# Two transformer blocks on one core: scores of two heads at a time, bias rows made ahead, compressed keys read by stride, the last group by halves of the tokens

## The chip, the cores and the metric

The kernel runs on 1 core of a Trainium2 chip. The metric is the device time of one execution in microseconds (us), a median of 3 runs. Everything below is of that core: TensorE (PE) does the matmuls and transposes, VectorE (DVE) and ScalarE (ACT) the work between them, GpSimd (POOL) fills a few tiles, and SyncE (SP) issues the DMAs from the chip's memory.

## What is computed

Two transformer blocks over 256 tokens of width 2048, batch 1, all in float32. The first has sparse attention with 16 query heads of 64 columns and 4 key heads beside a causal convolution of 31 taps over 1024 channels, both projected by one output matrix, and then a feed-forward network. The second block (latent attention, gated linear attention, a feed-forward network with a gated residual) isn't touched but for its last additions. Cut to what the change touches:

```
def compress_tokens(tok, pos, w1, w2):         # blocks of 32 tokens, one every 16: 15 blocks
    blocks = blocks + pos                      # pos: 32 vectors of 64
    return silu(flat @ w1) @ w2                # flat: 15 x (32*64); w1 2048x64; w2 64x64

proj = rms_norm(x) @ w_in                      # q, kv (3 branches), gates, conv_in
k_cmp, v_cmp = compress_tokens(...)            # branch 0
# per query head, branch in (compressed, selected, window):
s = q @ k.T * 64**-0.5 + rel_bias[bucket(t - s)]      # masked to s <= t
o += gate[branch] * softmax(s) @ v
conv = silu(layer_norm(depthwise_conv31(a * sigmoid(gate))))
x = x + concat([attn, conv]) @ w_out           # then the feed-forward network
...
x = x + gate_f * rms_norm(f, g_post_ffn)       # the last line of the second block
```

With 256 tokens the selected blocks and the window both cover every earlier token, so each head has two score matrices of 256 x 256 (causal) and one of 256 x 15 against the compressed keys.

## The kernel before

**Weights.** The work is a list of groups (`GROUPS`): projections `c0, c1, kvc, c2, kk, gt, q0, q1, c3, vv, q2, q3`, then the output projection in `oa0` to `oa7` (rows of the first four pairs of heads), `ob0` to `ob7` (rows of the last four pairs) and `oz0` to `oz7` (rows of the convolution), then the feed-forward network and block 2. A group is walked in steps (`MCS`), one weight tile of 128 x 1024 each. A tile lands as `raw`, ACT rounds it to `wh`, DVE takes the remainder `wl`, and PE does three matmuls per block of 128 rows: `wh` with the high part of the input, `wh` with the low part, `wl` with the high part. `run_group` writes these, and they are called main matmuls below; a step of `oa` or `ob` has 24 of them.

**Order.** The program is written out once, by a planner in Python that keeps a modelled clock per engine. Between main matmuls `tick()` lets side generators write their next piece when its model says that their inputs are ready; `need(n)` makes a generator wait for n of the eight PSUM banks. Each engine then runs its list in that order, whatever the real times are. `conv_gen`, the convolution on DVE, is a side with low priority: it is written where the model has DVE to spare.

**The pieces that the change touches.**
- `bias_gen` (L948) makes the relative bias on the chip: a one-hot table `oht` is loaded, one matmul gives 16 rows of 384 distances (`tabr`, sent to `dtab` in memory, read back by `load_B` as a tile `B` per pair), and 15 matmuls of 16 columns give the bias of the compressed keys (`cbias`).
- `cmp_gen`: per key and value, DVE writes the blocks with the position vectors added (`blk`, 8 additions, the even and odd tokens of a block in the two halves of the partitions), and 16 matmuls of 128 rows by 60 columns give the hidden layer.
- `ev_kk` copies the keys into `kz`, one tile per key head, with zeros in the 64 partitions that belong to the other head of a query pair. `att_gen(n)` does head n: two score matmuls of 128 rows against `kz` into two banks (`S1`, `S0`) and two against `kcz`; then DVE adds the bias and takes the maximum (`add_max`), ACT takes the exponentials, DVE the reciprocal sums `rs`, ACT scales P by them, PE transposes P (8 transposes), ACT copies them out (`PT`), and for a pair together PE multiplies with V (`PT,vz` and `PT,V`), in two halves of 64 columns of the array. ACT and DVE then write the pair's `o` as high and low part. `att_driver` starts head n when the scores of head n-1 are written.
- A main matmul of `ob0` to `ob7` is written only when its rows of `o` are planned; the fourth row block of each step is that of the last pair. `oz` needs the convolution's end: `sd`, `R` (the LayerNorm's factors), `upad` (swish), `ch` and `cl`.
- `finish()` ends the program: for each half of the tokens DVE adds, scales and writes four blocks of 512 columns and sends each to `out`.

Of the kernel before, what the change touches and what calls it, by code (L numbers as in the profile page):

```python
# [13 lines left out]
F32 = mybir.dt.float32  # L14
# [9 lines left out]
T = 256  # L24
D = 2048
# [118 lines left out]
PB = 3  # L144
# [4 lines left out]
AHEAD = 2  # L149
SKIP = 48  # L150
# [43 lines left out]
OH = Layout([("ohr", 384), ("ohf", 512)])  # L194
CA = Layout([("mix_g", 16), ("ffn_g", 16), ("relb", 16), ("cmask", 32), ("conv_w", 248), ("conv_b", 8), ("ln_g", 8),
# [3 lines left out]
OFF_C = 271  # L199
# [14 lines left out]
def _onehot(dist, width):  # L214
    o = np.zeros((128, width), np.float32)
    i = np.arange(len(dist))
    o[_bucket(dist), i] = 1.0
    o[32, i] = dist < 0
    return o


def pack_small(inp):
# [21 lines left out]
    for tt in range(2):  # L244
        cm[:, tt, :15] = (16 * np.arange(15)[None] + 31) <= (tt * 128 + t)[:, None]
    relb = np.zeros((33, 16), np.float32)
    relb[:32] = f["rel_bias"][:, HORD]
    relb[32] = NEG
    pos = f["cmp_pos"][0]
    oh = put(OH, dict(ohr=_onehot(np.arange(384) - 127, 384), ohf=_onehot(np.arange(512) - OFF_C, 512)))  # L250
    ca = put(CA, dict(
        mix_g=cols(f["mix_norm_g"][0]), ffn_g=cols(f["ffn_norm_g"][0]), relb=relb,
        cmask=cm.reshape(128, 32), conv_w=f["conv_w"][0].reshape(31, 8, 128).transpose(2, 1, 0).reshape(128, 248),
# [21 lines left out]
    w1 = w1.reshape(2, 16, 128, 64).transpose(0, 2, 1, 3).reshape(2, 128, 1024)  # L275
# [5 lines left out]
    return dict(vec=vec, fv=fv, oh=oh, ca=ca, cb=cb, w1=c(w1), wada=c(wada), x=c(x), pos=c(f["positions_2"]))  # L281
# [92 lines left out]
class Kern:  # L374
    def __init__(self, nc, tc, a, dump=None, stop=None):
# [11 lines left out]
        self.hl = {}  # L387
# [164 lines left out]
    def run_group(self, g):  # L552
# [5 lines left out]
        src = self.src  # L558
# [10 lines left out]
        kl = len(g["ks"]) - 1  # L569
# [3 lines left out]
        for mi in g["mcs"]:  # L573
# [6 lines left out]
            h, l = self.next_mc(mi)  # L580
            t["PE"] = max(t["PE"], self.l_end.pop(mi))
            for u in range(nt if g["mode"] == "w" else 2):
                o = ps[u][:min(n, 128)] if g["mode"] == "w" else ps[u][:, :n]
                for q, k in enumerate(m["ks"]):
                    xh, xl = src(k, N)
                    if g["mode"] == "w":
                        c = slice(q * n + u * 128, q * n + u * 128 + min(n, 128))
                        p = ((h[:, c], xh), (h[:, c], xl), (l[:, c], xh))
                    else:
                        c, ts = slice(q * n, q * n + n), slice(u * 128, u * 128 + 128)  # L590
                        p = ((xh[:, ts], h[:, c]), (xl[:, ts], h[:, c]), (xh[:, ts], l[:, c]))
                    for i, (a, b) in enumerate(p):
                        self.mm(o[:, :b.shape[1]], a, b, k == 0 and i == 0, k == kl and i == 2)
                    if q % GRAN == GRAN - 1 and (u, k) != (nb - 1, m["ks"][-1]):
                        self.tick()
            self.emitted += 1
            if mi != g["mcs"][-1]:
                self.tick()
        ev = self.evac[key]
# [5 lines left out]
        self.tick()  # L605

# [127 lines left out]
    def build(self):  # L734
        nc, tc = self.nc, self.tc
        with ExitStack() as es:
# [10 lines left out]
            with ExitStack() as ph:  # L747
# [12 lines left out]
                if not self.stop:  # L760
                    self.finish()
# [26 lines left out]
    def block1_setup(self):  # L788
# [12 lines left out]
        self.kz = P.tile([128, 4, 2, T], F32, name="kz")  # L801
        self.V = P.tile([128, 2, 2, 4, 64], F32, name="V")
        self.Gt = P.tile([128, 2, 8, 2, 3], F32, name="Gt")
        self.cbias = P.tile([128, 2, 8, 2, 16], F32, name="cbias")
        self.kcz = P.tile([128, 4, 16], F32, name="kcz")
# [6 lines left out]
        g.memset(self.kz, 0.0)  # L812
        g.memset(self.kcz, 0.0)
        g.memset(self.vz, 0.0)
        g.memset(self.cbias, NEG)
# [26 lines left out]
        self.side(self.bias_gen())  # L842
# [105 lines left out]
    def bias_gen(self):  # L948
        while "ss" not in self.flags:
            yield  # L950
        oh = self.early.tile([128, OH.n], F32, name="oht", tag="g2")
        self.sy.dma_start(oh, self.a["oh"])
        ohr, ohf = (oh[:33, o:o + n] for o, n in OH.at.values())
        yield 8.0
        yield from self.need(1)
        o = self.bank()
        self.mm(o[:16, :384], self.ca("relb", 0, 16)[:33], ohr)
        yield
        tr = self.early.tile([16, 384], F32, name="tabr", tag="tok")
        self.act(tr, o[:16, :384], AF.Copy)  # L960
        self.free(o)
        self.dtab = self.dp.tile([16, 384], F32, name="dtab")
        self.sy.dma_start(self.dtab, tr)
        yield
        yield from self.need(1)
        bk = self.bank()
        o = bk[:, :256].rearrange("p (n h) -> p n h", n=16)
        for w in range(15):
            c = OFF_C - 31 + 128 - 16 * w
            self.mm(o[:, w], ohf[:, c:c + 128], self.ca("relb", 0, 16)[:33])  # L970
        yield

        for tt, w, n in ((0, 8, 7), (1, 0, 15)):
            self.v.tensor_copy(self.cbias[:, tt].rearrange("p a u n -> p (a u) n")[:, :, :n],
                               o[:, w:w + n].rearrange("p n h -> p h n"))
        self.free(bk)
# [1059 lines left out]
```

## Time and profile before

| what | value |
|---|---|
| median of the runs | 2206.18 us (2204.81 to 2206.24) |
| the profiled execution | 2205.54 us, its span 2203.8 us |
| PE | busy 2167.6 us, 98% of the span, 17465 records |
| DVE | busy 1692.8 us, 77% |
| ACT | busy 1179.5 us, 54% |
| DMA | 499.20 MB, 227 GB/s on average |

A busy time counts every record of an engine, so PE at 98% says that PE nearly always had something in it, not that it couldn't be given less. One fp32 matmul shows as two records, a main matmul as one. A group of equal records that follow each other is printed as one row with its count; its time reaches from the first start to the last end, and the ends of records overlap the next start by some 0.1 us, so what something costs PE is read from start to start. All rows name line 306, a helper that records each call, so pieces are told apart by their tiles.

### The profile page before, as it was taken

What the parts mean: (1) busy time and instruction counts of PE and PEld (TensorE: products, weight loads), DVE (VectorE), ACT (ScalarE), POOL (GpSimd) and SP (SyncE); (2) the same over time, 40 slices, a digit from 0 to 9 for tenths busy, and PEclk for the clock granted to TensorE, in tenths of its full rate; (3) what the DMA queues carried; (4) which work ended last, traced back from release to release, by engine and by line L of the source; (5) the groups of instructions that cost most, each with busy time, mean ns of one, the idle gap of its engine ahead of it and who ended that gap; (6) DMA issues with size and microseconds to landing.
All of it is one profiled execution on the core that took longest, in us unless ns stands there. A gap on an engine that the chain in (4) does not pass through costs nothing.

```text
span 2203.8 us, 42192 instructions
## 1 busy us (share of the span) xinstructions
PE 2167.6 (98%) x17465; PEld 2081.5 (94%) x17465; DVE 1692.8 (77%) x2611; ACT 1179.5 (54%) x1805; POOL 5.1 (0%) x18
## 2 busy tenths in 40 slices
PE   8999999999999999999999999999999999999997
PEld 7998889999999999999999889989998999899986
DVE  7998988999998699999988666678676665554455
ACT  5447686655553355555556664466444444444443
POOL 0000000000000000000000000000000000000000
PEclk9999999999999999999999999999999999999999
DMA  6554325788888788888855334646776775555553
GB/s 232 192 178 152 130 82 194 254 322 325 310 326 323 276 316 316 323 319 306 302 201 180 134 134 137 209 153 211 251 260 244 254 252 189 194 188 176 192 194 131
DMA packets 86784, 499.20 MB, mean 227 GB/s; under 512 B 9648, under 2 KB 12096, under 8 KB 40128
## 3 DMA queue, kind: packets, MB, share of 16 engines
q1 hardware_dynamic: 86592, 496.51, 63.6%
q8 instruction: 136, 2.23, 0.4%
q14 instruction: 56, 0.46, 0.1%
HBM read 494.35 MB, written 2.12 MB: 225 GB/s over the span
## 4 chain that ended last, share of the span: by engine, by line
PE 89%; DVE 6%; ACT 2%; issue 1%; DMA 1%; SPq 0%; DVEq 0%; ACTq 0%
PE ps L306 89%; DVE wl L306 2%; DMA raw<-in_wst_dram 1%; DVE cacc L306 1%; ACT wh L306 0%; DVE X L306 0%; DVE ac L306 0%; ACT L306 0%; DVE og L306 0%; ACT P L306 0%; DVE nt L306 0%; ACT X L306 0%; ACT ge L306 0%; DVE XT L306 0%; DVE ss L306 0%
## 5 line engine op out<-in xcount | busy, mean ns | idle before, releaser
L306 PE MATMUL ps<-X,wh 128*128 128x256 f32 (+1 forms) x7680 | 1330.3, 277 | 5.1 <-ACT X L306 2.9
L306 ACT ACTIVATE wh<-raw 128x1024 fp32r<-128x1024 f32 (+2 forms) x741 | 782.8, 1058 | 837.6 <-PE ps L306 781.2
L306 DVE TENSOR_TENSOR wl<-raw,wh 128x1024 fp32r<-128x1024 f32 (+2 forms) x741 | 898.9, 1215 | 393.8 <-PE ps L306 339.4
L306 PEld LDWEIGHTS ps<-X,wh 128*128 128x128 f32 x7680 | 1161.5, 188 | 11.4 <-ACT X L306 3.5
L306 PE MATMUL ps<-X,wl 128*128 128x256 f32 (+1 forms) x3840 | 1060.2, 276 | 4.8 <-DVE wl L306 4.8
L306 PEld LDWEIGHTS ps<-X,wl 128*128 128x128 f32 x3840 | 722.1, 188 | 6.0 <-DVE wl L306 6.0
L306 DVE SCALAR_TENSOR_TENSOR ac<-wa,cs,ac 128x512 f32<-128x512 f32 x360 | 269.5, 749 | 6.8
L306 PE MATMUL ps<-hid,wh 128*128 128x256 f32 x1408 | 239.5, 275 | 0.0
L306 PE MATMUL ps<-wh,hid 128*128 128x512 f32 x704 | 216.5, 388 | 0.0
L306 PEld LDWEIGHTS ps<-hid,wh 128*128 128x128 f32 x1408 | 212.0, 188 | 0.0
L306 PE MATMUL ps<-hid,wl 128*128 128x256 f32 x704 | 193.6, 275 | 0.0
L306 PEld LDWEIGHTS ps<-wh,hid 128*128 128x128 f32 x704 | 131.9, 188 | 27.4
L306 PE MATMUL ps<-wl,hid 128*128 128x512 f32 x352 | 136.6, 388 | 0.0
L306 PEld LDWEIGHTS ps<-hid,wl 128*128 128x128 f32 x704 | 132.2, 188 | 0.0
L306 DVE SCALAR_TENSOR_TENSOR cacc<-upad,cat,cacc 128x256 f32<-128x256 f32 x240 | 99.6, 476 | 0.3 <-ACT cacc L306 0.2
L306 PEld LDWEIGHTS ps<-wl,hid 128*128 128x128 f32 x352 | 66.1, 188 | 13.5
L306 DVE SCALAR_TENSOR_TENSOR y<-vt,fv,y 128x256 f32<-128x256 f32 x176 | 73.3, 478 | 0.0
L306 PE MATMUL ps<-wh,X 128*128 128x512 f32 x192 | 60.7, 397 | 0.0
L306 ACT ACTIVATE y<-ps,fv 128x256 f32<-128x256 f32 x84 | 49.3, 587 | 0.0
L306 PE MATMUL ps<-o,wh 128*128 128x256 f32 x256 | 46.8, 283 | 1.2 <-ACT o L306 1.1
L306 ACT ACT_TABLE_LOAD x30 | 38.5, 1283 | 9.9 <-DMA XT<-in_x_dram 4.9
L306 PEld LDWEIGHTS ps<-wh,X 128*128 128x128 f32 x192 | 35.3, 188 | 6.6
(321 smaller groups left out, 1726.7 us busy)
## 6 DMA issues: line engine op xcount, KB each, us to landing
raw<-in_wst_dram SPq DMA_DIRECT2D x363, 1024.0 KB, 4.9
wa<-in_wada_dram SPq DMA_DIRECT2D x192, 512.0 KB, 6.9
raw<-in_wst_dram SPq DMA_DIRECT2D x4, 768.0 KB, 4.5
raw<-in_wst_dram SPq DMA_DIRECT2D x4, 512.0 KB, 5.4
B<-dtab SPq DMA_DIRECT2D x8, 256.0 KB, 5.2
out_dram<-og SPq DMA_DIRECT2D x8, 256.0 KB, 2.7
XT<-in_x_dram SPq DMA_DIRECT2D x3, 512.0 KB, 6.8
w<-in_w_dram SPq DMA_DIRECT2D x2, 512.0 KB, 5.7
```

The source lines that it names most:

```text
L306: return f(*x, **k)
```

## The change

1. `bias_gen` is gone with its table, its 16 matmuls, the trip through `dtab` and the tile `cbias`. The bias rows come ready as an input and `load_B` reads them from there. The bias of the compressed keys is read as a strided piece of `B` by `add_max`, over the 7 and 15 columns that exist.
2. `cmp_gen` writes no `blk`. 64 matmuls per key and value (32 tokens of a block, two halves of 64 partitions each) read `tok` by stride, 34 columns at a time: two column blocks of 16 + 1, where the 17th column is the position vector, whose result is then the bias of the silu. `w1` is loaded once into each half of the partitions, four loads of 512 KB in place of two.
3. Keys are kept as they are (`kk`, `kc2`). `score_gen(p)` writes the scores of both heads of a pair, one from partitions 0 to 63 and one from 64 to 127, when four banks are free; `att_gen` takes the banks over, and the pair's second head waits for the flag `M` that the first head sets after its maxima. `PB`, the number of P tiles, goes from 3 to 4.
4. The last group holds its last three steps (`TAIL`): their matmuls for the first half of the tokens come first, then those for the second half; `last_add` and `last_scale` end each half by itself, in pieces of 256 columns, in place of `finish()`.

```diff
-PB = 3
+PB = 4
+TAIL = 3
...
+            us = range(nb)
+            if n_mc >= ends:
+                held.append((m, hl))
+                us = (0,)
...
+        if held:
+            self.later(lambda: self.last_add(0, ps[0]), False)
+            for m, hl in held:
+                for q in range(len(m["ks"])):
+                    self.products(g, ps[1], 1, m, q, hl, N)
+                    self.tick()
+            self.later(lambda: self.last_add(1, ps[1]), False)
...
-            for l in range(16):
-                self.mm(o[:64, :60], self.w1[:, l], self.blk[:, l].rearrange("p a n -> p (a n)"), l == 0, l == 15)
...
+            for l in range(32):
+                for u in range(2):
+                    t = self.tok[64 * u:64 * u + 64, 2 * kv]
+                    x = bass.AP(tensor=t.tensor, offset=t.offset + l, ap=[list(t.ap[0]), [T + 32, 2], [16, 17]])
+                    self.mm(o[u][:64, :34].rearrange("p (b n) -> p b n", b=2), self.w1[kv][64 * u:64 * u + 64, l], x, l == 0, l == 31)
...
-        yield from self.need(2)
-        S1, S0 = self.bank(), self.bank()
-        self.mm(S1, q[:, 128:], self.kz[:, h].rearrange("p r s -> p (r s)"))
...
+        yield from self.need(4)
+        S = [(self.bank(), self.bank()) for _ in range(2)]
+        rows = [slice(64 * u, 64 * u + 64) for u in range(2)]
+        for u, r in enumerate(rows):
+            self.mm(S[u][0], q[r, 128:], self.kk[r, b].rearrange("p r s -> p (r s)"))
+        for u, r in enumerate(rows):
+            self.mm(S[u][1][:, 0:256].rearrange("p (r s) -> p r s", r=2), q[r, :128], self.kk[r, b, :, :128])
+        for tt in range(2):
+            for u, r in enumerate(rows):
+                self.mm(S[u][1][:, 256 + 16 * tt:271 + 16 * tt], q[r, tt * 128:tt * 128 + 128], self.kc2[r, b, 0:15])
...
+        while u and f"M{n - 1}" not in self.flags:
+            yield
...
+    def last_add(self, tt, ps):
...
+        f = self.f[:, tt, 1536:]
+        q = self.f2.tile([128, 512], F32, name="q", tag="u")
+        for e in range(2):
+            c = slice(256 * e, 256 * e + 256)
+            self.tt(f[:, c], ps[:, c], f[:, c], OP.add)
+            self.act(q[:, c], f[:, c], AF.Square, accum_out=self.ssq[:, tt, 3 + e:4 + e])
+        self.last_f = self.f2.tile([128, 512], F32, name="lf", bufs=2), *getattr(self, "last_f", ())
+        self.tt(self.last_f[0], f, self.gpb[1][:, 1], OP.mult)
+        if tt:
+            self.last_scale(0, (2, 3), self.last_f[1])
...
+        self.last_scale(tt, range(4) if tt else (0, 1), self.last_f[0])
```

The planner writes the rest of the program in another order as well. Three places show what stands where.

PE before, at the end of the attention: transposes of the last head's P (numbered P tiles are one head's), the convolution's sums (`upad`), the last pair's matmuls with V, then main matmuls of `ob0`.

```order
L306 MATMUL ps<-vecs,P_3725 128x128
L306 MATMUL ps<-vecs,P_3724 128x128 x2
L306 MATMUL ps<-upad,vecs 128x256 x2
L306 MATMUL ps<-PT,vz 64x256 x2
L306 MATMUL ps<-PT,V 64x256 x2
L306 MATMUL ps<-PT,V 64x128 x2
L306 MATMUL ps<-PT,V 64x256 x2
L306 MATMUL ps<-PT,V 64x128 x2
L306 MATMUL ps<-o,wh 128x256 x2
L306 MATMUL ps<-o,wl 128x256
```

PE now, at the same place, from the last main matmul of `oa7` on: V of the last pair but one, the transposes of both heads of the last pair (the first head's P are 3772 and 3773, the second's 3821 and 3822), V of the last pair, `ob0`.

```order
L298 MATMUL ps<-o,wl 128x256
L298 MATMUL ps<-PT,vz 64x256 x2
L298 MATMUL ps<-PT,V 64x256 x2
...
L298 MATMUL ps<-vecs,Pc_1889 128x128 x2
L298 MATMUL ps<-vecs,P_3773 128x128
L298 MATMUL ps<-vecs,P_3772 128x128 x2
...
L298 MATMUL ps<-vecs,Pc_1890 128x128 x2
L298 MATMUL ps<-vecs,P_3822 128x128
L298 MATMUL ps<-vecs,P_3821 128x128 x2
...
L298 MATMUL ps<-PT,vz 64x256 x2
...
L298 MATMUL ps<-o,wh 128x256 x2
```

Before, 30 main matmuls stand between the transposes of the last two heads, and the convolution's first sums ahead of the last V. Now no main matmul stands from V of pair 6 to the end of V of pair 7: the 1872 main matmuls up to `oa7` are all written before, and both of the convolution's sums before the transposes of head 13.

ACT before, from the last head's exponentials on: they, its scaling, the copies of the transposes of both heads, and then the convolution's first steps.

```order
L306 ACTIVATE P_3724,sm<-P_3724,mx 128x256 x2
L306 ACTIVATE P_3725,sm<-P_3725,mx 128x128 x2
L306 ACTIVATE sc,sm<-sc,mx 128x16 x2
L306 ACTIVATE P_3724<-P_3724,rs 128x256 x2
L306 ACTIVATE P_3725<-P_3725,rs 128x128 x2
L306 ACTIVATE o<-ps 128x256
L306 ACTIVATE PT<-ps 128x512 x2
L306 ACTIVATE wh<-raw 128x1024
L306 ACTIVATE PT<-ps 128x512 x2
L306 ACTIVATE sd<-ps 128x256
L306 ACTIVATE upad<-cacc_93 128x4x256
```

ACT now, from the second half of the last head's exponentials on.

```order
L298 ACTIVATE sc,sm<-sc,mx 128x15
L298 ACT_TABLE_LOAD
L298 ACTIVATE upad<-cacc_93,cat 128x256 x4
L298 ACTIVATE o<-ps 128x256
L298 ACTIVATE PT<-ps 128x512 x2
L298 ACTIVATE P_3821<-P_3821,rs 128x256 x2
L298 ACTIVATE P_3822<-P_3822,rs 128x128 x2
L298 ACTIVATE ch<-upad 128x1024
L298 ACTIVATE upad<-cacc_94,cat 128x256 x4
L298 ACTIVATE PT<-ps 128x512 x2
L298 ACTIVATE ch<-upad 128x1024
L298 ACTIVATE o<-ps 128x256
```

A table load, the swish of both halves of the convolution (`upad`) and two roundings (`ch`) stand between the last head's exponentials and the copy of its `o`; before, they stood behind all of it.

## Rows read from the trace of the kernel before

**Rows 1.** The chain of waits: start, us, engine, tile, count (four of its pieces)

```profile
34.98 70.52 PE ps L306 x592
...
253.36 44.13 PE ps L306 x339
...
307.12 1.49 ACT P L306 x4
...
317.75 2.37 DVE cacc L306 x2
```

**Rows 2.** Busy time by stretch: length, then PE, PEld, DVE, ACT, POOL, clock, DMA share

```profile
161.70:319.10 157.40, 154.80 (x1142) 135.02 (x1141) 140.58 (x442) 121.27 (x342) 0.00 (x0) 1.00 0.39 131
319.10:345.90 26.80, 24.24 (x199) 23.14 (x198) 20.83 (x28) 19.01 (x24) 0.00 (x0) 1.00 0.33 109
```

**Rows 3.** PE in order of time at the bias matmuls: start, us, tiles, count

```profile
46.56 0.81 PE L306 MATMUL ps<-oht,cat 33*16 33x384 f32 x2
...
48.91 3.52 PE L306 MATMUL ps<-cat,oht 33*128 33x16 f32 x30
...
54.10 0.63 PE L306 MATMUL ps<-X,wh 128*128 128x256 f32 x2
...
54.74 0.63 PE L306 MATMUL ps<-X,wh 128*128 128x256 f32 x2
```

**Rows 4.** PE in order of time at the compressed keys, first of two such bursts

```profile
102.50 2.08 PE L306 MATMUL ps<-blk,w 128*64 128x60 f32 x32
```

**Rows 5.** DMA issues of the page: tile, count, KB each, us to landing

```profile
w<-in_w_dram SPq DMA_DIRECT2D x2, 512.0 KB, 5.7
```

**Rows 6.** PE in order of time at one head's scores and one pair's V

```profile
282.34 1.45 PE L306 MATMUL ps<-kz,qT 128*128 128x512 f32 x4
...
283.99 0.48 PE L306 MATMUL ps<-o,wh 128*128 128x256 f32 x2
...
284.88 0.65 PE L306 MATMUL ps<-PT,vz 128*64 128x256 f32 x4
...
286.76 0.50 PE L306 MATMUL ps<-o,wh 128*128 128x256 f32 x2
```

**Rows 7.** DVE in order of time at the attention's end

```profile
303.25 1.23 DVE L306 TENSOR_TENSOR wl<-raw,wh 128x1024 fp32r<-128x1024 f32 x1
...
326.87 1.75 DVE L306 RECIPROCAL R<-sd 128x256 f32<-128x256 f32 x1 [1.94 <-ACT sd L306]
```

**Rows 8.** ACT in order of time at the attention's end

```profile
303.99 0.50 ACT L306 ACTIVATE P<-P,mx 128x256 f32<-128x256 f32 x1
...
306.24 0.20 ACT L306 ACTIVATION_READ_ACCUMULATOR sc<-sc,mx 128x1 f32 x1
...
308.51 1.06 ACT L306 ACTIVATE PT<-ps 128x512 f32<-128x512 f32 x2
...
325.06 1.28 ACT L306 ACT_TABLE_LOAD   x1 [2.63 <-PE ps L306]
...
331.52 2.08 ACT L306 ACTIVATE upad<-cacc,cat 128x256 f32<-128x256 f32 x4 [2.44 <-DVE cacc L306]
...
335.41 1.05 ACT L306 ACTIVATE ch<-upad 128x1024 fp32r<-128x1024 f32 x1
```

**Rows 9.** PE in order of time at the start of the group after the attention

```profile
319.58 0.39 PE L306 MATMUL ps<-o,wh 128*128 128x256 f32 x2
...
319.92 0.39 PE L306 MATMUL ps<-o,wh 128*128 128x256 f32 x2
...
321.53 0.84 PE L306 MATMUL ps<-o,wh 128*128 128x256 f32 x2 [1.11 <-ACT o L306]
```

**Rows 10.** PE and DVE in order of time at the program's end

```profile
2191.66 0.39 PE L306 MATMUL ps<-wl,hid 128*128 128x512 f32 x1
...
2193.55 2.74 DVE L306 SCALAR_TENSOR_TENSOR og<-og,sd,XT 128x512 f32<-128x512 f32 x4
...
2197.06 2.74 DVE L306 SCALAR_TENSOR_TENSOR og<-og,sd,XT 128x512 f32<-128x512 f32 x4
```

More of the change, by code (lines that the diff above doesn't have):

```diff
@@ L572, in run_group @@
         t = self.clock.t
-        for mi in g["mcs"]:
+        ends = len(g["mcs"]) - (TAIL if g is GROUPS[-1] else 0)
+        held = []
+        for n_mc, mi in enumerate(g["mcs"]):
             m = MCS[mi]
@@ L946, in conv_gen @@
             self.flags.add(f"conv{b}")
[L948 to L976, printed above, removed]
-    def ev_kvc(self, ps):
-        self.tok = self.early.tile([128, 4, T], F32, name="tok")
-        self.w1 = self.early.tile([128, 16, 64], F32, name="w1", tag="g1")
-        self.blk = self.early.tile([128, 16, 4, 15], F32, name="blk", tag="g2")
+    def ev_kvc(self, ps):
+        self.tok = self.early.tile([128, 4, T + 32], F32, name="tok")
+        self.w1 = [self.early.tile([128, 32, 64], F32, name=f"w1{kv}") for kv in range(2)]
+        for kv in range(2):
+            for u in range(2):
+                self.sy.dma_start(self.w1[kv][64 * u:64 * u + 64].rearrange("p l f -> p (l f)"), self.a["w1"][kv])
+            pos = self.ca("pos", 32 * kv, 32)
+            self.act(self.tok[:, 2 * kv:2 * kv + 2, T:], pos[:, None, :].to_broadcast([128, 2, 32]), AF.Copy)
         for j in range(4):
-            self.tt(self.tok[:, j], ps[j][:, :T], self.R, OP.mult)
+            self.tt(self.tok[:, j, :T], ps[j][:, :T], self.R, OP.mult)
         self.side(self.cmp_gen())
@@ L1033, in ev_kk @@
             for b in range(2):
[L1034 to L1036 removed]
+                self.tt(self.kk[:, b, br], ps[2 * br + b][:, :T], self.R, OP.mult)
         self.flags.add("kk")
@@ L1105, in att_driver @@
         self.done, self.PT = 0, {}
-        for n in range(16):
-            while f"q{n // 2}" not in self.flags or n >= PB and f"T{n - PB}" not in self.flags or \
-                    n and f"S{n - 1}" not in self.flags:
+        for p in range(8):
+            while f"q{p}" not in self.flags or 2 * p + 1 >= PB and f"T{2 * p + 1 - PB}" not in self.flags or \
+                    p and f"M{2 * p - 1}" not in self.flags:
                 yield
-            self.side(self.att_gen(n))
-            yield ATT
+            self.side(self.score_gen(p))
+            yield 2 * ATT
         while self.done < 16:
@@ L1145, in att_gen @@
         rs = A.tile([128, 2, 3], F32, name="rs", bufs=6)
+        cmp = [sc[:, tt, :(7, 15)[tt]] for tt in range(2)]
         for r in range(2):
@@ L1149, in att_gen @@
             self.add_max(P0[:, r], S0[:, 128 * r:128 * r + 128], rev(B, 128), mx[:, 0, r + 1:r + 2])
-        self.tt(sc, S0[:, 256:288].rearrange("p (t n) -> p t n", t=2), self.cbias[:, :, p, u], OP.add)
-        self.v.tensor_reduce(mx[:, :, 0], sc, axis=AX, op=OP.max)
+        for tt, c in enumerate(cmp):
+            bias = bass.AP(tensor=B.tensor, offset=B.offset + 96 + 128 * tt, ap=[list(B.ap[0]), [-16, c.shape[1]]])
+            self.add_max(c, S0[:, 256 + 16 * tt:256 + 16 * tt + c.shape[1]], bias, mx[:, tt, 0:1])
         self.v.tensor_scalar(mx, mx, -1.0, None, op0=OP.mult)
         self.free(S1, S0)
+        self.flags.add(f"M{n}")
         if u == 0 and p < 7:
@@ new lines, in last_scale @@
+    def last_scale(self, tt, js, last):
+        x = self.XT.rearrange("p (c a) t -> p c (a t)", a=2)
+        for j in js:
+            o = self.f[:, tt, 512 * j:512 * j + 512]
+            f = last if j == 3 else o
+            self.stt(o.rearrange("p (c n) -> p c n", c=2), f.rearrange("p (c n) -> p c n", c=2), self.rt[tt],
+                     x[:, 2 * j:2 * j + 2, 256 * tt:256 * tt + 256], OP.mult, OP.add)
+            self.sy.dma_start(self.a["out"][128 * tt:128 * tt + 128, 512 * j:512 * j + 512], o)
```

150 lines of the change are left out of this document (58 added, 92 removed).

## The prediction

> **What bounds the kernel now.** I read the windows first, then the chain of waits, then the engines in order of time where the chain leaves PE. PE is the bound where it has no gap, and a matmul taken away is then worth its time: so it is ahead of the attention, where the chain runs through PE without a break from 34.98 to 105.5 [rows 1]. In the attention (161.7 to 319.1 us) PE is busy 154.8 of 157.4 us, but DVE is busy 140.6 and ACT 121.3 [rows 2]: whoever shortens PE's list there by over ten us meets DVE. And the chain shows where the attention really ends: PE until 297.5, then DVE and ACT pieces, among them the scaling of a head's P [rows 1]. Of each step of `ob0`, three row blocks can go ahead of the last pair; the fourth waited for the last pair's `o`, and PE stood there 1.1 us before 321.53 [rows 9]. So the last pair's softmax, not PE's list, sets when the output projection gets on. The stretch behind it, 319.1 to 345.9, runs at 26.8 us for 192 main matmuls [rows 2]; three of them take 0.34 us at full clock [rows 9], 21.8 us for all, so 5.0 us there are waits for weights and for `o`, behind a convolution that DVE and ACT are still ending. After PE's last matmul, DVE works on alone [rows 10].
>
> The profiled execution took 2205.54 us, of which 2203.8 are its span; the median of the runs is 0.6 above it. I sum against 2205.54 and add 0.6 at the end. A measurement of this kernel tells some 0.2% (4.4 us) from no change.
>
> **The bias matmuls.** Gone are one burst of 0.8 and one of 3.5 us [rows 3], less an overlap of 0.1: -4.2. After the second burst five triples of main matmuls start 0.64 us apart, not 0.34 [rows 3, 9]: the lower level of PE's clock after 30 tiny matmuls. That goes too: 5 x 0.30 = -1.5. The bias tile now comes straight from an input with an unchanged number of loads, and nobody waits longer for that: 0. The strided `add_max` on 7 and 15 columns takes the place of an addition and a maximum; both are small pieces of DVE's list, and I take 0 with half a us either way.
>
> **The compressed keys.** Two bursts of 2.08 us go [rows 4]: -4.2. In each, 16 matmuls of 60 columns (32 records) took 0.13 us apiece. A matmul of 16 columns is no faster: 30 records in 3.5 us are 0.117 a record against 0.065 [rows 3, 4], so at these sizes it isn't the columns that set the time, and I give a matmul of 34 columns 0.13 us too. There are 128 of them. If the two halves of the partitions run side by side, this is 64 x 0.13 = 8.3 us, if one after the other 16.6; if columns did count (34 of 60) and they run side by side, 4.7. I take 8.3: V's matmuls, two halves of the array's columns, do run side by side, since 12 records of 256 columns and 8 of 128 took 1.88 us [rows 6], where at the scores' rate (two records each of 512 and of 256 columns with the compressed keys' in 1.65 us) they would take over three. That is a row on column halves; none is on row halves. The Trainium skill (TensorEngine Tiling (Array Packing), Theoretical Speedup) gives up to 2x where the contracted dimension is at most 64; no run here shows it yet, and by it this term would be 8.3, without it 16.6.
>
> A burst of over 4 us of tiny matmuls may lower the clock as the bias burst did; the bursts of 2.08 us were not followed by it. I count one of the two with +1.5 (bounds 0 and +3.0). The tiles of `w1` are four loads in SP's queue, 5.7 us to land [rows 5], asked for when `kvc` is evacuated; 48 main matmuls (5.4 us) lie between that and the first burst in the new order. I take a wait of 1.0 (0 to 5.7, the whole landing). The 16 additions on DVE that go are no gain here, since this stretch is PE's.
>
> Up to the first scores: -4.2 - 1.5 - 4.2 + 8.3 + 1.5 + 1.0 = **+0.9** (from -4 to +15).
>
> **The scores.** A head's scores take PE 1.65 us (282.34 to 283.99) [rows 6], 16 heads 26.4. Side by side a pair takes what a head took, with 0.2 for coming and going between modes: 8 x 1.85 = 14.8, so PE is relieved of 11.6 us. I take none of it as such. DVE has only 16.8 us of gaps in this stretch [rows 2], some of them inside the softmax chains. The new order has it do the convolution's first LayerNorm pieces, 2.37 us for the means [rows 1] and about as much for the squares, ahead of the last pair, where before they came behind it; ACT's squares and a table load move with them. So PE's saving turns into waits for DVE, and I take the last pair's `add_max` to end where it did, at 303.25 (bounds: up to 8 us earlier, or 1 later).
>
> What follows is longer. Before: from the end of head 14's `add_max` at 303.25 [rows 7] to the start of `ob0` at 319.1, 15.85 us. Its pieces on the path (two heads' exponentials of 2.45, two scalings of 1.49, three copies of transposes of 1.06, one rounding of a weight tile, as long as `ch` at 1.05, one `o`, 0.4 by the 0.50 for as many columns of P, and V's 1.88 [rows 1, 6, 8]) make 14.4, so 1.5 us go into handovers. Now ACT's list, read from the order, between the same two points is: exponentials 2.45, `PT` 1.06, scaling 1.49, exponentials 2.45, table load 1.28, `upad` 2.08, `o` 0.4, `PT` 1.06, scaling 1.49, `ch` 1.05, `upad` 2.08, `PT` 1.06, sum 17.95 [rows 1, 8]; then V 1.88. Ahead of the first exponentials stand now a rounding and a table load that wait for the sums of the convolution; they start about 1.5 late. And the first scaling waits for DVE, which has `R` (1.75), `wl` (1.23) [rows 7] and head 15's `add_max` ahead of it; that falls into the time that ACT needs anyway, within 0.2. With 2.0 for handovers, since there are more: 17.95 + 1.88 + 1.5 + 0.2 + 2.0 = 23.5, **+7.7**.
>
> All this time PE has nothing but transposes and V, so the clock falls, as it does after the bias burst: V's 1.88 takes twice that on the path, **+1.9** (0 to 2.5), and the first five triples after it 0.30 longer each, **+1.5** (0 to 1.6).
>
> **Behind the attention.** The convolution is then done and the weights of the next steps are rounded (11 `wh` in a row on ACT), so the 192 main matmuls take their 21.8 and not 26.8: **-5.0** (bounds -5.0 and 0, should another wait come up). The `oz` steps find their rows ready, as they did.
>
> **The end.** Before, 7.7 us lie between PE's end at 2192.05 and DVE's at 2199.80, with two runs of four scalings of 2.74 each [rows 10]. Now the first half of the tokens is added while PE works on the second (18 main matmuls of 512 columns), and two of its four scalings too. Left are the additions of the second half and its factor, 1.5 before (2192.05 to 2193.55) and, by pieces, perhaps 0.7 more, two scalings of the first half (1.37) and four of the second (2.74): 6.1 to 6.4. **-1.3** (bounds 0 and -3).
>
> **Sum.** 0.9 + 7.7 + 1.9 + 1.5 - 5.0 - 1.3 = +5.7. 2205.5 + 5.7 + 0.6 = 2211.8; I say **2212**.
>
> **The rivals.**
> *The scores' saving arrives.* The heads start earlier by what PE saves, and the last pair with them: 11.6 less, 2200, from 2194 to 2202. For it: the chain of waits is PE's up to 297.5 [rows 1]. Against: DVE's 140.6 of 157.4 us [rows 2], to which the convolution's pieces come. It decides if the last `add_max` ends over 9 us before where it did.
> *The long last pair costs about what the rest saves.* The clock stays up (the three terms of 1.5, 1.9 and 1.5 fall away), or the last pair begins 4 or 5 us earlier: 2207, from 2202 to 2208. For it: no row here has PE idle for so long between V and main matmuls. Against it: the drop in [rows 3].
> *Row halves take turns.* Slower than my forecast: the compressed keys cost 8.3 more, and the scores give PE nothing back, which costs up to 6 more where DVE would have had time: 2218 to 2228. For it: no row here has two row halves in flight. Against it: the column halves do run side by side [rows 6].
>
> **How the numbers follow.** Forecast (2208 to 2217) 0.56, the saving arrives 0.12, equal 0.20, row halves take turns 0.12. The range from 2202 to 2222 leaves out most of the first rival and the upper part of the third. Faster by over 0.2% (below 2201.8): 0.12. Within: the second rival and the lower part of the forecast up to 2210.6, 0.20 + 0.17 = 0.37. Slower: 0.39 + 0.12 = 0.51.
>
> **What would show it.** In the trace of the changed kernel: no bias rows near 46 to 52 us; two bursts on `tok` of about 4.2 us each, with starts in pairs a few ns apart (8 us each: row halves take turns); score bursts of 1.65 to 1.9 us a pair; head 14's `add_max` ending near 304; PE nearly empty for some 18 us ahead of the first main matmul of `ob0` near 329, with a granted clock below 1.00 there; some 23 us from there to the next group; DVE's last scaling some 6.4 us after PE's end. I am wrong if PE goes on without that gap, which would mean that the last pair came early; if the gap is 6 us or less; or if the sum of the stretch up to the first scores is off by more than 4 us.

## The result and the profile after

The changed kernel takes 2223.97 us (median of 4 runs, 2219.65 to 2226.66), against 2206.21 on the same chips: 1.0077 times as long, interval 1.0060 to 1.0093. That is slower, as forecast, and by 12 us more. The profiled execution took 2226.66, the longest of the four; its span is 2224.9 us, 21.1 more than before.

Main matmuls are the same 16344 in both programs, so one can be found by its number in either trace, and the difference of its start is what has been won or lost by then. Number 576 is the last landmark ahead of the compressed keys, 1104 lies ahead of the first scores, 1872 is the first of `ob0`, 2208 lies in the feed-forward network, 16343 is the last.

| from main matmul to main matmul | forecast | after, us against before |
|---|---|---|
| start to 576 (bias) | -5.7 | -6.5 |
| 576 to 1104 (compressed keys) | +6.6 | +13.0 |
| 1104 to 1872 (attention) | +9.6 | +17.8 |
| 1872 to 2208 (output projection) | -3.5 | -4.6 |
| 2208 to the last (feed-forward, block 2) | 0 | +3.0 |
| last to the end | -1.3 | -1.5 |

**The compressed keys.** PE in order of time, columns as in [rows 4]; the last row is the second key and value.

```profile
90.23 0.28 PE L298 MATMUL ps<-tok,w 64*64 64x34 f32 x2 [1.66 <-DMA w<-in_w_dram]
92.56 7.04 PE L298 MATMUL ps<-tok,w 64*64 64x34 f32 x126 [2.05 <-DMA w<-in_w_dram]
...
100.33 0.63 PE L298 MATMUL ps<-X,wh 128*128 128x256 f32 x2
...
100.97 0.63 PE L298 MATMUL ps<-X,wh 128*128 128x256 f32 x2
...
106.95 4.07 PE L298 MATMUL ps<-tok,w 64*64 64x34 f32 x128
```

The first burst waits twice for `w1`, 3.7 us. Its other 126 records then take 7.04 us; the second burst, 128 such records, takes 4.07 and waits for nothing. Behind the first, eight triples are slow, seven of them 0.64 apart as in [rows 3]. The window from 88 to 106 us shows it as a granted clock of 0.62 (columns as in [rows 2]), and the page gives the loads (columns as in [rows 5], which had 5.7 us to landing):

```profile
88.00:106.00 18.00, 14.29 (x166) 13.79 (x164) 7.68 (x17) 3.90 (x6) 0.00 (x0) 0.62 0.59 146
```

```profile
w<-in_w_dram SPq DMA_DIRECT2D x4, 512.0 KB, 10.4
```

**The attention's end.** DVE in order of time: the end of head 14's maxima, which stood at 303.25 in [rows 7], `R`, and then the pieces behind a wait for `o`.

```profile
317.55 0.17 DVE L298 TENSOR_SCALAR mx<-mx 128x6 f32<-128x6 f32 x1
318.25 1.75 DVE L298 RECIPROCAL R<-sd 128x256 f32<-128x256 f32 x1 [0.53 <-ACT sd L298]
...
331.48 0.42 DVE L298 TENSOR_TENSOR o<-ps,o 128x256 fp32r<-128x256 f32 x1 [5.72 <-ACT o L298]
331.82 0.18 DVE L298 RECIPROCAL rs<-sm 128x6 f32<-128x6 f32 x1
...
335.91 1.22 DVE L298 TENSOR_TENSOR cacc<-cacc,R 128x1024 f32<-128x1024 f32 x1
```

ACT in the same stretch, what answers to [rows 8]:

```profile
320.69 0.51 ACT L298 ACTIVATE P<-P,mx 128x256 f32<-128x256 f32 x1
...
327.81 1.28 ACT L298 ACT_TABLE_LOAD   x1
329.10 2.07 ACT L298 ACTIVATE upad<-cacc,cat 128x256 f32<-128x256 f32 x4
331.08 0.36 ACT L298 ACTIVATE o<-ps 128x256 fp32r<-128x256 f32 x1
...
332.30 1.49 ACT L298 ACTIVATE P<-P,rs 128x256 f32<-128x256 f32 x4
333.69 1.05 ACT L298 ACTIVATE ch<-upad 128x1024 fp32r<-128x1024 f32 x1
337.17 2.07 ACT L298 ACTIVATE upad<-cacc,cat 128x256 f32<-128x256 f32 x4 [2.43 <-DVE cacc L298]
```

And PE, what answers to [rows 6, 9]: the last pair's scores, its second head's transposes, its V, `ob0`.

```profile
314.73 1.56 PE L298 MATMUL ps<-kk,qT 64*128 64x512 f32 x8
316.12 0.52 PE L298 MATMUL ps<-kc,qT 64*128 64x15 f32 x8
316.57 1.13 PE L298 MATMUL ps<-upad,vecs 128*128 128x256 f32 x4
...
332.61 0.66 PE L298 MATMUL ps<-vecs,Pc 128*128 128x128 f32 x2 [5.98 <-DVE Pc L298]
...
339.77 0.69 PE L298 MATMUL ps<-PT,vz 128*64 128x256 f32 x1 [3.64 <-ACT PT L298]
...
343.38 0.74 PE L298 MATMUL ps<-o,wh 128*128 128x256 f32 x2
```

A pair's scores take 1.84 us (314.73 to 316.57) where one head's took 1.65 [rows 6], so the halves of the partitions run side by side. The swish of the convolution stands on ACT ahead of `o`, on `o` DVE waits before it can make head 15's `rs`, and on that PE waits 6 us. The second swish waits for DVE and holds the copy of `PT` behind it. From the end of the maxima, 317.6, to `ob0` it is 25.8 us, where it was 15.85.

PE's waits between main matmuls 1104 and 1872 are 20.5 us together, where they were 2.6. The longest ahead of the last pair stands in the middle, and half clock behind it (0.50 granted from 218 to 222 us), with triples of 512 columns starting 1.28 apart instead of 0.68:

```profile
218.62 0.79 PE L298 MATMUL ps<-wl,X 128*128 128x512 f32 x1 [3.62 <-DVE wl L298]
219.21 1.05 PE L298 MATMUL ps<-wh,X 128*128 128x512 f32 x2
...
220.49 1.05 PE L298 MATMUL ps<-wh,X 128*128 128x512 f32 x2
```

**The end.** DVE's last scalings, what answers to [rows 10]: they end 6.2 us after PE's end at 2214.67, 7.7 before.

```profile
2218.13 2.08 DVE L298 SCALAR_TENSOR_TENSOR og<-og,r,XT 128x512 f32<-128x512 f32 x3
2220.13 0.75 DVE L298 SCALAR_TENSOR_TENSOR og<-lf,r,XT 128x512 f32<-128x512 f32 x1
```

### The profile page after: what moved, and what is told of

Read it like the earlier page. It is cut to its first block, busy times and chain, and to the rows that moved or that the text cites. A ratio compares the mean times of both kernels' runs of the same rounds, so it can differ in the third digit from the quotient of the medians.

```text
span 2224.9 us, 42516 instructions
## 1 busy us (share of the span) xinstructions
PE 2172.1 (98%) x17625; PEld 2085.5 (94%) x17625; DVE 1681.3 (76%) x2625; ACT 1179.7 (53%) x1811; POOL 2.8 (0%) x15
## 4 chain that ended last, share of the span: by engine, by line
PE 86%; DVE 7%; ACT 4%; DMA 1%; issue 1%; SPq 0%; DVEq 0%; ACTq 0%
PE ps L298 86%; DVE wl L298 2%; ACT P L298 1%; DVE cacc L298 1%; ACT wh L298 1%; DVE P L298 0%; DMA w<-in_w_dram 0%; ACT L298 0%; DVE X L298 0%; DMA raw<-in_wst_dram 0%; DMA wa<-in_wada_dram 0%; ACT X L298 0%; DVE nt L298 0%; ACT ge L298 0%; ACT upad L298 0%
## 5 line engine op out<-in xcount | busy, mean ns | idle before, releaser
L298 PEld LDWEIGHTS ps<-X,wh 128*128 128x128 f32 x7680 | 1163.4, 188 | 11.3 <-ACT X L298 3.4
L298 PE MATMUL ps<-wl,X 128*128 128x512 f32 x96 | 38.7, 403 | 3.6 <-DVE wl L298 3.6
## 6 DMA issues: line engine op xcount, KB each, us to landing
w<-in_w_dram SPq DMA_DIRECT2D x4, 512.0 KB, 10.4
```

The costliest lines, as they stand in the source:

```text
L298: return f(*x, **k)
```

## The experiments

The same stretches for every kernel that ran, in us against the profiled execution before. The first 240 main matmuls are a column of their own: they differ by up to 3.7 us from trace to trace, whatever the kernel, so kernels are compared by the other columns. Each kernel has one trace. How far the attention's column can be trusted shows in three kernels that have the same order there on PE, ACT and DVE, instruction by instruction (changed, `w1_early`, `w1_128`): 17.8, 16.4 and 17.8, so some 1.5 us there mean nothing. The last column is the median of so many runs; a single run is the profiled one.

On the names: `w1_early` and `w1_128` are the changed kernel with other loads of `w1`. `w1_conv` is `w1_early` with the convolution's LayerNorm held until the last head's maxima are asked for (flag `M15`), `w1_heads` is `w1_early` with the heads' scores one by one as before, `w1_heads_conv` both. `taps_pairs` and `taps_heads` are `w1_conv` and `w1_heads_conv` with less convolution. `bias_tail` is the kernel before with the ready bias and the last group by halves alone, `bias_tail_conv` the same with the convolution held. `blk` is the changed kernel with the compressed keys as before. An `_m` at the end: the planner's prices for ACT corrected in the attention.

| kernel | to 240 | 240-576 | 576-1104 | 1104-1872 | 1872-2208 | 2208-last | end | us of the runs |
|---|---|---|---|---|---|---|---|---|
| changed | -0.2 | -6.3 | 13.0 | 17.8 | -4.6 | 3.0 | -1.5 | 2224.0 (4) |
| w1_early | 0.7 | -6.3 | 3.5 | 16.4 | -4.9 | 2.7 | -1.5 | 2215.4 (4) |
| w1_128 | -2.6 | -6.3 | 9.4 | 17.8 | -4.7 | 3.0 | -1.7 | 2220.5 (1) |
| w1_conv | -2.3 | -6.3 | 3.5 | 8.1 | -2.6 | 2.8 | -1.6 | 2207.2 (1) |
| w1_heads | 0.5 | -6.3 | 3.5 | 26.1 | -4.9 | 3.2 | -1.6 | 2226.1 (1) |
| w1_heads_conv | -1.8 | -6.3 | 3.5 | 9.8 | -2.9 | 1.3 | -1.6 | 2207.5 (1) |
| taps_pairs | -0.2 | -6.3 | 3.5 | 10.4 | -2.9 | 1.4 | -1.5 | 2209.8 (1) |
| taps_heads | 0.4 | -6.3 | 3.5 | 15.8 | -4.4 | 0.6 | -1.5 | 2213.7 (1) |
| w1_early_m | -0.1 | -6.3 | 3.5 | 7.6 | -3.8 | 1.0 | -1.6 | 2205.8 (1) |
| w1_conv_m | -0.5 | -6.3 | 3.5 | 3.8 | -3.5 | 1.1 | -1.5 | 2201.9 (10) |
| bias_tail | 0.2 | -6.3 | 0.2 | 11.3 | -2.5 | 0.2 | -1.7 | 2206.9 (10) |
| bias_tail_conv | 0.2 | -6.3 | 0.2 | 11.9 | -3.3 | -0.1 | -1.8 | 2204.2 (10) |
| bias_tail_conv_m | -2.6 | -6.3 | 0.2 | 2.2 | 0.6 | -0.1 | -1.7 | 2198.5 (7) |
| blk | -2.1 | -6.3 | 0.2 | 3.9 | -3.5 | 0.7 | -1.7 | 2196.7 (5) |
| blk_m | -3.0 | -6.3 | 0.2 | 4.6 | -3.5 | 0.5 | -1.8 | 2197.8 (6) |

### The loads of w1

```diff
-    def ev_kvc(self, ps):
-
-        self.tok = self.early.tile([128, 4, T + 32], F32, name="tok")
+    def pre_kvc(self):
         self.w1 = [self.early.tile([128, 32, 64], F32, name=f"w1{kv}") for kv in range(2)]
...
                 self.sy.dma_start(self.w1[kv][64 * u:64 * u + 64].rearrange("p l f -> p (l f)"), self.a["w1"][kv])
+
+    def ev_kvc(self, ps):
+
+        self.tok = self.early.tile([128, 4, T + 32], F32, name="tok")
...
```

> The changed kernel with one edit: the four loads of w1 are issued at the start of the group kvc instead of at its evacuation, some 21 us earlier. In the changed kernel the first burst on tok waits 3.7 us for them, runs its 128 records in 7.0 us where the second takes 4.1, and eight triples of main matmuls behind it start 0.64 us apart instead of 0.34 (2.4 us). Theory (the late load is the whole trouble there: the wait lowers the clock, and the burst itself doesn't): all three go, 3.7 + 2.9 + 2.4 = 9.0 us less up to the first scores, both bursts near 4.1 us, and about 2215 in all. Rival (the burst of tiny matmuls lowers the clock by itself, as the bias burst did): only the 3.7 goes, and half clock stays in or behind the first burst, about 2220.

Both bursts now take 4.07 us and wait for nothing, and the stretch falls from 13.0 to 3.5:

```profile
89.38 4.07 PE L298 MATMUL ps<-tok,w 64*64 64x34 f32 x128
...
98.29 4.08 PE L298 MATMUL ps<-tok,w 64*64 64x34 f32 x128
```

The theory holds: 2215.4 us, ratio to before 1.0044 (1.0027 to 1.0060). Here the clock falls with the wait, not with the burst. A wait isn't needed everywhere: in the kernel before, the 30 tiny matmuls of the bias follow a main matmul without one, and half clock came behind them [rows 3].

```profile
48.71 0.28 PE L306 MATMUL ps<-X,wl 128*128 128x256 f32 x1
```

The stretch is still 3.3 us longer than in the kernels that keep the old compressed keys (3.5 against 0.2): two bursts of 4.07 for two of 2.08.

```diff
-    w1 = w1.transpose(0, 2, 1, 3).reshape(2, 64, 2048)
+    w1 = np.concatenate([w1.transpose(0, 2, 1, 3).reshape(2, 64, 2048)] * 2, 1)
...
-            for u in range(2):
-                self.sy.dma_start(self.w1[kv][64 * u:64 * u + 64].rearrange("p l f -> p (l f)"), self.a["w1"][kv])
+            self.sy.dma_start(self.w1[kv].rearrange("p l f -> p (l f)"), self.a["w1"][kv])
```

> The changed kernel with one edit: w1 comes twice in memory, once per half of the partitions, and is loaded by two DMAs over all 128 partitions (1024 KB each) in place of four over 64 partitions (512 KB each); issued where the changed kernel issues them, the same bytes. Theory (a load over 64 partitions runs at half the rate, and that is why the first burst waits): the first of them lands some 5 to 7 us after its issue instead of 10.4, the wait ahead of the first burst falls from 3.7 to under 1 us, the burst takes 4.1 us, and the stretch is 8 to 9 us shorter. Rival (it is late because two times the bytes stand in the queue at that place, whatever their form): it waits 2 us or more, and the clock falls again.

Neither quite. The loads land in 8.1 us, PE waits 1.4, and the clock falls even so: the burst takes 6.11. So the form of the load is part of it. That twice the bytes at that place are the rest is likely (two loads of 512 KB took 5.7 [rows 5]), but no run shows it by itself. A wait of 1.4 us was enough to lose 2.0 us in the burst and some 2.4 behind it.

```profile
87.56 6.11 PE L298 MATMUL ps<-tok,w 64*64 64x34 f32 x128 [1.36 <-DMA w<-in_w_dram]
```

### Pairs, and the convolution's place

First the convolution held, in `conv_gen` ahead of its first sums:

```diff
         yield
+        while "M15" not in self.flags:
+            yield
         yield from self.need(1)
```

> The kernel with the early w1 loads and one edit more: the convolution's LayerNorm and swish are not written before the maxima of the last head (flag M15). Theory (the convolution's end, put ahead of and between the last pair's steps on ACT and DVE, makes the last pair late and long): from the end of head 14's add_max to the first main matmul of ob0 it takes 16 to 18 us instead of 25.8, the add_max ends 3 to 5 us earlier, and 5 us come back behind, where the convolution's end runs beside the output projection as before: 5 to 9 us less than with the early loads alone. Rival (the pairs themselves fill the queues of DVE and ACT, whatever the convolution does): the add_max ends where it did within 2 us, and the total moves by less than 4 us.

The attention falls from 16.4 to 8.1 and 2.3 come back behind it; without the first column that is 6.0 less in all, within the 5 to 9 of the theory. From the maxima's end at 303.7 to `ob0` at 322.1 it is 18.4 us, as the theory has it; that the maxima themselves would come 3 to 5 us earlier failed: 4.1 by the traces, but 3.0 of that is the runs' different start.

```diff
-PB = 4
+PB = 3
...
-        for p in range(8):
...
-            self.side(self.score_gen(p))
-            yield 2 * ATT
+            self.side(self.att_gen(n))
+            yield ATT
...
-        yield from self.need(4)
-        S = [(self.bank(), self.bank()) for _ in range(2)]
...
+        yield from self.need(2)
+        S1, S0 = self.bank(), self.bank()
+        self.mm(S1, q[r, 128:], self.kk[r, b].rearrange("p r s -> p (r s)"))
```

> The kernel with the early w1 loads and one edit: heads one by one again, each as soon as the scores of the head before are written and two banks are free, with three P tiles, from the 64 partitions of its keys (no zero padding, no two heads side by side). All else is as changed. Theory (a pair's two softmaxes, written as one batch, make the weight tiles wait on DVE and ACT, and the last pair late): PE is 11 us busier with scores, yet the wait for wl near 215 us goes, head 14's add_max ends 5 to 8 us earlier, the gap ahead of ob0 shrinks below 5 us of waits, and the total is 6 to 12 us less than with the early loads alone. Rival (the convolution's place is what matters and it keeps it): the total moves by less than 4 us or rises by the scores' 11 us.

The theory fell, by one run: without pairs the attention takes 9.7 us more.

> Both edits on the kernel with the early w1 loads: heads one by one and the convolution's LayerNorm after the last head's maxima. This is the attention's end as in the kernel before, with the bias, the compressed keys and the last group as changed. If both the pairs and the convolution's place matter, it is the fastest of the four, near the kernel before less the bias (6.5) and the end (1.5), plus the bursts of the compressed keys (8.2 for 4.2): about 2202. If only one matters, it equals the better of the two single edits within 2 us.

2207.5, as much as `w1_conv`: the convolution's place is what costs in both, and PE's 11 us of scores seemed to be worth only 1.7 (9.8 against 8.1), hardly more than equal orders differ by; over the whole program, without the first column, nothing is left of it.

### Is DVE the bound?

The same kernels with 60 tap operations of the convolution left out (the output then lacks them):

```diff
-            for k in range(31):
+            for k in range(31 if i < 2 else 16):
```

> Pairs, early w1 loads, convolution's LayerNorm held, and 60 of the 240 tap operations of the convolution on DVE (taps 16 to 30 of four of its eight channel blocks) left out, so the convolution's part of the output lacks them: 28.6 us of DVE's work less, nearly all of it in the attention. Theory (with pairs, DVE's queue is what PE waits for): the attention from the first scores to ob0 gets 8 to 14 us shorter. Rival (the pairs' chain of softmax steps between ACT, DVE and PE sets the time, DVE's load doesn't): less than 4 us.

> The same 60 operations left out of the kernel with heads one by one, early w1 loads and the convolution's LayerNorm held. Theory (one by one, PE is the bound but for the last head, and DVE's load only decides the end): 2 to 5 us less. Rival (DVE is the bound in both): as much as with pairs, 8 to 14 us.

DVE is busy 22.0 us less (1680.6 to 1658.6 with pairs; the 28.6 expected add up 60 durations that overlap), and the attention got longer, by 2.3 with pairs (8.1 to 10.4) and by 6.0 with heads (9.8 to 15.8). No theory had that, and each ran once. With the work the order that the planner wrote had changed too, so these two runs don't tell whether DVE is the bound. They led to the planner's prices: it takes 0.29 us for an exponential of 256 columns, which starts 0.49 after the one before in the trace.

```diff
             c = 0.06 + n * 0.9e-3
+            if self.att:
+                c += 0.11 * any(hasattr(k.get(i), "tensor") for i in ("scale", "bias")) + 0.1 * ("accum_out" in k)
```

> Pairs with early w1 loads and the convolution's LayerNorm held, and one edit in the planner: in the attention its price of an ACT instruction gets 0.11 us more where scale or bias is a tile, and 0.10 more where a sum is accumulated, near what the traces show (0.49 and 0.39 us per exponential where the model had 0.29 and 0.18). No instruction is added or taken away, only the order. With it pair 7's scores stand at main matmul 1794, not 1848. Theory (PE waits in the attention because the planner, with prices too low for ACT, writes transposes and V ahead of what is ready): PE's waits between the first scores and ob0 fall from 16 us to 8 or less, and the total by 5 to 9 us against the kernel without this edit, to near 2200. Rival (ACT and DVE are simply full): under 2 us.

> The same edit of the planner's prices with the early w1 loads alone, the convolution's LayerNorm not held. If the prices alone are the cause of the attention's loss, the planner now finds the right place for the convolution too, and the total is within 3 us of the kernel with both edits. If the place of the convolution is a cause of its own, it stays 5 us or more above it, and from head 14's add_max to ob0 it still takes over 22 us.

> The planner's prices corrected in the kernel with ready bias and last group by halves alone (heads one by one, compressed keys as before, the convolution's LayerNorm held). Without this edit the 6 us won ahead of the scores were lost again in the attention, where PE waited 9 us for ACT's PT and P near its end. Theory (wrong prices): PE's waits there fall below 5 us and the total to 2196 to 2200. Rival (the last softmax chain is the end of the attention, whatever the order): within 2 us of 2204.

The same instructions in another order: the attention falls by 4.3 us with the convolution held (8.1 to 3.8), by 8.8 with it free (16.4 to 7.6), and by 9.7 with heads (11.9 to 2.2, of which 3.9 come back behind). `w1_conv_m` takes 2201.9, ratio 0.9981 (0.9971 to 0.9991); its ten runs lie between 2197.5 and 2205.7, and `w1_conv` ran once, so the 4.3 of the traces say more than the totals. In `w1_early_m` one can see what the order did to the last pair: the maxima of head 14 end 145.8 us after main matmul 1104 (at 153.35), in `w1_early` 153.7 (1104 at 154.14), in the kernel before 146.9. The rows of `w1_early` and of `w1_early_m`:

```profile
307.72 0.17 DVE L298 TENSOR_SCALAR mx<-mx 128x6 f32<-128x6 f32 x1
```

```profile
299.06 0.17 DVE L298 TENSOR_SCALAR mx<-mx 128x6 f32<-128x6 f32 x1
```

What PE waited for between 160 and 325 us, first in `w1_conv`, then in `w1_conv_m` (us in total, times, longest):

```profile
PE ps L298 <- DVE Pc L298: 5.5, 2, 5.1
PE ps L298 <- DVE wl L298: 3.6, 1, 3.6
PE ps L298 <- ACT P L298: 2.7, 3, 1.8
PE ps L298 <- ACT PT L298: 1.2, 1, 1.2
PE ps L298 <- DVE XT L298: 1.1, 1, 1.1
PE ps L298 <- DVE mx L298: 0.7, 1, 0.7
```

```profile
PE ps L298 <- ACT PT L298: 5.5, 3, 2.9
PE ps L298 <- DVE wl L298: 3.7, 1, 3.7
```

14.8 us became 9.2; that is more than the 8 that were expected at most. The wait of 3.7 for `wl` stays; the table load ahead of it on ACT is still not in the prices. The convolution's place is a cause of its own only in part: free, it costs 3.8 us more with the right prices (7.6 against 3.8), where it cost 8.3 with the wrong ones. That lies between the two cases expected of `w1_early_m`; from head 14's maxima to `ob0` it still takes 24.6 us there.

`bias_tail_conv_m` takes 2198.5, ratio 0.9970 (0.9959 to 0.9981), as its theory had it, and PE's waits up to `ob0` fall to 4.2 us:

```profile
PE ps L298 <- DVE Pc L298: 2.7, 1, 2.7
PE ps L298 <- ACT P L298: 0.7, 2, 0.5
PE ps L298 <- ACT PT L298: 0.4, 1, 0.4
PE ps L298 <- DVE upad L298: 0.2, 1, 0.2
PE ps L298 <- DVE qT L298: 0.2, 1, 0.2
```

### Parts of the change alone

> The kernel before with two parts of the change alone, the ready bias (with the strided maxima over 7 and 15 columns) and the last group by halves of the tokens; compressed keys by additions and 16 matmuls, zero-padded keys, heads one by one and three P tiles as before; the convolution's LayerNorm is held until the last head's maxima, which is about where it stood. By the parts as measured, 6 us less up to the first scores and 1.5 less at the end: 2198.5 to 2200, faster than both kernels. Rival (what PE saves early is lost in the attention, as in the changed kernel): 2203 to 2206.

> Ready bias and last group by halves alone, heads one by one, compressed keys as before, nothing held: it differs from the kernel with the compressed keys undone (2196.7) by the pairs alone (side by side scores, four P tiles). In the order the convolution's first sums stand at main matmul 1842, ahead of the last pair's V, where with the pairs they stand at 1872. Theory (PE's saving by the pairs arrives once the last pair is clear of the convolution): 2203 to 2208, 7 to 11 us more than with the pairs. Rival (the pairs are worth little, the undone compressed keys all): within 3 us of 2196.7.

Ready bias and the last group alone, in `bias_tail_conv` with the convolution held, in `bias_tail` without. Both win 6.1 us ahead of the scores by the table and lose 11 to 12 in the attention, of which some 3 come back behind it. They take 0.9996 (0.9987 to 1.0006) and 1.0007 (0.9997 to 1.0016) of the time before, no difference. The 2198.5 to 2200 expected of `bias_tail_conv` failed and its rival held; for `bias_tail` the 2203 to 2208 of the theory came true.

`blk` is the changed kernel with `cmp_gen`, `ev_kvc` and the layout of `w1` as before.

> The changed kernel with one part undone: the compressed keys by DVE's additions and 16 matmuls of 128 rows by 60 columns, w1 loaded as before; ready bias, pairs with four P tiles and the last group by halves stay. DVE's 16 additions are back, so the planner has less of DVE to spare and writes the convolution's LayerNorm after the last pair's scores by itself: its first sums stand at main matmul 1872 in the order, not at 1782. Theory (the late w1 loads and the convolution's place made the loss): 6 us less up to the first scores, no wait of 3.7 us, the last pair's steps without swish between them, 1.5 less at the end: 2198 to 2204. Rival (the pairs themselves cost): 2206 or more.

2196.69 us, 0.9965 (0.9951 to 0.9978) of before, 27 us less than the changed kernel, faster than both. Its edit differs from that of `bias_tail` by the pairs alone, with their four P tiles; the order differs as well. Its median is 10.2 us lower, by the ratios to before it is 9.3, by the table without the first column 7.9: against that order most of the 11.6 that the pairs save PE arrives here. Its waits up to 325 us:

```profile
PE ps L298 <- ACT PT L298: 6.1, 2, 3.1
PE ps L298 <- DVE mx L298: 1.9, 2, 1.3
PE ps L298 <- DVE XT L298: 1.4, 1, 1.4
PE ps L298 <- ACT P L298: 1.1, 2, 0.6
PE ps L298 <- DVE qT L298: 1.0, 1, 1.0
PE ps L298 <- DVE wl L298: 0.5, 1, 0.5
PE ps L298 <- DVE Pc L298: 0.2, 1, 0.2
```

12.2 us up to `ob0`, where `bias_tail` has 10.2 up to its own, 4.9 of them in one wait for `Pc`. Against heads in a better order little of the saving is left: `bias_tail_conv_m` has 4.2 us of waits, and its ratio to before, 0.9970, is not told apart from 0.9965 here. By the table without the first column it is 1.6 us behind `blk` and 1.2 behind `blk_m`.

> The changed kernel with the compressed keys undone, and the planner's ACT prices corrected in the attention. In the kernel with the undone compressed keys PE still waits 13 us between the first scores and ob0, of them 6.1 for PT at the end. If wrong prices are a cause there too, 3 to 6 us less, near 2192. If that kernel's waits are the last pair's chain of softmax steps alone, which no order shortens, within 2 us of 2196.7.

2197.83, ratio 0.9969 (0.9958 to 0.9981), the same: here the corrected prices change nothing, and the 3 to 6 us did not come.

## Why the prediction was right or wrong

- **The bias**, -5.7: -6.3 in every kernel. Right.
- **The compressed keys**, +6.6: +13.0. The bursts were sized rightly, 4.07 us each against 4.15, and the rival in which row halves take turns is out: the second burst's records start in pairs, 6 ns apart or less and some 60 from pair to pair, where [rows 4]'s single records start 58 or 59 apart; and a pair's scores take 1.84 us where one head's took 1.65. There the rule of the Trainium skill (TensorEngine Tiling (Array Packing), Theoretical Speedup), up to 2x for a contracted dimension of 64, agrees with the trace. The step that failed is the wait for `w1`. I let 5.4 us of main matmuls cover a landing of 5.7 us and took 1.0; the loads of 64 partitions landed in 10.4. And I gave the lower clock 1.5 us as something that a burst does by itself. The runs show it behind a wait, and then it takes 3.0 us in the burst and some 2.4 behind it. My upper bounds, 5.7 and 3.0, were for each alone; that one brings the other wasn't in the sum.
- **The scores**: 1.84 us per pair against 1.85. Right.
- **The start of the last pair**, taken as unchanged: 14.4 us later, 6.5 of them from the stretch before, 7.9 from the attention. This is the larger miss. The step that failed: I read the order around the last pair, but took its place in time from the trace of before. I held that DVE is nearly full there, so PE's saving turns into waits for it. PE's saving did turn into waits, but a full DVE isn't what makes them: DVE is busy 147.5 of 179.2 us in `w1_early`, and 147.3 of 165.0 in `bias_tail_conv_m`. The runs show the order in its place: `w1_early` has the changed kernel's order in the attention, and another order of the same work moves the maxima of head 14 from 153.7 to 145.8 us behind main matmul 1104. The planner, whose model lets ACT's exponentials take little more than half of their time, had put transposes, V and the convolution's end ahead of what was ready. That its prices made this order rests on three kernels in which the stretch falls by 4.3 to 9.7 us with better ones; in `blk` it doesn't fall.
- **The last pair's path**, 23.5 and V at half clock, 25.4: 25.8. Right in its pieces: ACT's list, table load, two swishes and two roundings included, and V with 3.6 us (339.77 to 343.38) at half clock. `w1_conv` takes most of them out and gets 18.4.
- **The clock behind the gap**, +1.5: only the first triple of `ob0` is slow (343.38 to 344.08), some 0.4.
- **Behind the attention**, -5.0: 22.1 us for the 192 main matmuls (343.38 to 365.52), -4.6 in the table. Right.
- **The end**, -1.3: -1.5. Right.
- **Not in the sum**: 3.0 us in block 2, in two places, 2.2 where DVE waits for a load of `wa` that is issued near 1127 us, and 0.8 near 1486. It is 2.7 to 3.2 in five kernels with the new compressed keys, 0.6 to 1.4 in five others, and -0.1 to 0.7 in those with the old ones. What makes it was not tried and stays open.

The forecast sign was right, and its mechanism at the attention's end too; two terms, 6.4 and 8 us too small, carried the time out of the range. One of the prediction's own signs of being wrong came: up to the first scores the sum is +6.5 where +0.9 stood, more than 4 off. That the time falls between the 2218 and 2228 of the rival of row halves is chance, since that mechanism is out.

## What to carry to other kernels

When a change makes an operand come from a new load, find where its load stands in the queue and in which form: the wait on PE is paid again in the clock. When a program's order is written by a model, a change of any part reorders all the rest; undo each part by itself, and in more than one order, before judging one, and hold the model's prices against the trace: here, by the table without the first column, the pairs were worth 10.1 us (`w1_heads` against `w1_early`), nothing (the same with the convolution held), 7.9 (`bias_tail` against `blk`) or 1.2 (`bias_tail_conv_m` against `blk_m`).

## What the runs showed of the hardware

- Loads over 64 partitions in pieces of 512 KB took 9.9 to 10.4 us to landing in all nine kernels that had four of them, early or late in the queue; two over 128 partitions with 1024 KB each took 8.1, and two of 512 KB over 128 partitions 4.5 to 5.7.
- The same burst of 128 records took 4.07 or 4.08 us at full clock in every trace where PE didn't wait ahead of it, and 6.11 and 7.04 (126 of the records) behind waits of 1.4 and 3.7 us, with the granted clock at 0.64 and 0.62 of those stretches.
- Matmuls of 64 rows in the two halves of the partitions run side by side: a pair's scores took 1.84 us, one head's over 128 rows 1.65.
